# Modulation products in steps of four, and one weight split for two k-tiles

## The chip, the cores and the metric

The kernel runs on one core of one Trainium2 chip. The metric is device time in microseconds (us) per execution. The engines named below are TensorE (PE, with its weight loads PEld), VectorE (DVE), ScalarE (ACT), GpSimd (POOL) and the queue of SyncE (SP), which issues nearly all loads.

## The reference, cut to what matters

Two transformer blocks are applied to 256 rows of 2048 numbers, in float32. The first block has two layers; each multiplies normalised rows by a wide input matrix, runs three kinds of attention and multiplies by an output matrix. Its rows are modulated first, by a scale and a shift that come from two conditioning vectors:

```python
shift, scale, gate = jnp.split(sc @ w_ada[l] + b_ada[l], 3, axis=-1)
shift_c, scale_c, gate_c = jnp.split(scc @ w_ada[l] + b_ada[l], 3, axis=-1)
h = rms(x, norm_w[l]) * (1.0 + scale[:, None]) + shift[:, None]
hc = rms(xc, norm_w[l]) * (1.0 + scale_c) + shift_c
u = h @ w_in
```

So the first layer's scale and shift need two rows (`sc` and `scc`, each of 2048 numbers) times 2048 x 4096 weights, before the first dense product. The second block is a mixer, a cross attention and a feed-forward layer, all of them dense products of 256 rows with wide matrices.

## The kernel before, in words

**Dense products.** A weight matrix comes in chunks of at most 512 columns, and a chunk in blocks of two k-tiles (a k-tile is 128 rows). `weights` (line 388) loads one block of 128x1024 numbers on the SP queue into a `raw` tile, of which there are three. Each k-tile is then split in two: `split` (line 374) writes `hi` on ScalarE (line 376) and `lo` = raw - hi on VectorE (line 377). There are four `hi` tiles and four `lo` tiles of 128x512, so four k-tiles can be held. `dense` (line 403) streams the split weights and holds the activations still, `denseT` (line 429) holds the weights still and streams the activations; both make three products for each k-tile and token tile or column tile (lines 420 to 422, and 440, 442, 443). With 512 tokens (four token tiles: the first layer and the keys of the second) a block is 24 products of 512 columns. With 256 tokens it is 12 products of up to 512 columns in `dense`, or 24 of 256 columns in `denseT`; that is the second layer's queries, and all of the second block. Results leave PSUM through an `evac` function at the end of a chunk.

**The first products.** `first_products` (line 1310) works through the 16 k-tiles of the first three chunks of `w_in` in five parts of 2, 2, 4, 4 and 4 k-tiles (`PARTS`), since a part of the rows can be normalised as soon as its scale and shift are known. While the dense products of one part run, the modulation of the next part is made by `ada_pe` (line 601): 16 steps, one for each k-tile of `w_ada`, and an `end`. A step loads the weights of one k-tile and makes two products (shift and scale) at line 629. The stationary operand is 32 columns wide (the two conditioning vectors and zeros), so a product uses one of four groups of 32 columns of the array, and its result goes to the 32 PSUM partitions that belong to the group: `q = 64 * (kt % 2) + 32 * b`. The products are 256 columns long in the first two parts (the two lie side by side in one loaded tile) and 512 in the last three (one loaded tile each). The loaded tiles are those of the attention's `PT`, five of them. The steps of the first part are called directly in `block1`, between the loads of `x` and `ctx` (line 1371).

**What sets the order.** `push` queues jobs and `tick` starts them at a pace in modelled TensorE time; in `first_products` one job starts every `n * len(chunks) * 2.56 / FIRST` us of it. A scheduler then puts the instructions of each engine in a fixed order, also the SP queue's loads; at run time each engine works through its list and waits where an operand or a buffer is not free.

Of the kernel before, what the change touches and what calls it, by code (L numbers as in the profile page):

```python
# [11 lines left out]
F32R = mybir.dt.float32r  # L12
# [2 lines left out]
AX = mybir.AxisListType  # L15

UNITS = 50
FIRST = 20
D = 2048
NKT = D // 128  # L20
EPS = 1e-6
# [121 lines left out]
class Weights:  # L143


    def __init__(self, ap, name):
        self.ap, self.at, o = ap, {}, 0
        rows, chunks = CHUNKS[name]
        for ch in chunks:
            self.at[tuple(ch)] = o  # L150
            o += rows * sum(n for _, n in ch)
# [41 lines left out]
class K:  # L193
# [8 lines left out]
    def __init__(self, ctx, tc, a):  # L202
        self.tc, self.nc, self.a = tc, tc.nc, a
        nc = self.nc
        self.jobs, self.running, self.next = [], [], 0.0
        self.urgent, self.asked, self.unext = [], 0, 0.0
        self.side, self.side_rate, self.side_credit = [], 0.0, 0.0
        self.now, self.late = 0.0, []
        self.const = ctx.enter_context(tc.tile_pool(name="const", bufs=1))
        self.str = ctx.enter_context(tc.tile_pool(name="stream", bufs=3))  # L210
        self.up = ctx.enter_context(tc.tile_pool(name="units", bufs=1))
        self.sm = ctx.enter_context(tc.tile_pool(name="small", bufs=8))
        self.ps = ctx.enter_context(tc.tile_pool(name="psum", bufs=1, space=bass.MemoryType.PSUM))
        self.nu = self.alt = 0
        self.vt = self.const.tile([128, NVT], F32, name="vt")
        nc.scalar.dma_start(self.vt, a["vt"])
        n = CS["tri"][0]
        self.cs = self.const.tile([128, n], F32, name="cs")
        nc.scalar.dma_start(self.cs, a["cst"][:, :n])
        self.flip = self.const.tile([128, 128], F32, name="flip")  # L220
        nc.scalar.dma_start(self.flip, a["flip"])
        self.ident = self.const.tile([128, 128], F32, name="ident")
        make_identity(nc, self.ident)
        self.ones = self.const.tile([128, 128], F32, name="ones")
        nc.vector.memset(self.ones, 1.0)
        self.mhalf = self.const.tile([128, 16], F32, name="mhalf")
        nc.vector.memset(self.mhalf, -0.5)
# [161 lines left out]
    def weights(self, w, k0, pieces):  # L389

        nc = self.nc
        raw = self.str.tile([128, 2, 512], F32, name=self.name("raw"), tag="raw", bufs=3)
        n, src = w.block(k0, pieces)
        nc.sync.dma_start(raw[:, :, :n], src)
        out = []
        for j in range(2):
            hi = self.str.tile([128, 512], F32R, name=self.name("hi"), tag="hi", bufs=4)
            lo = self.str.tile([128, 512], F32R, name=self.name("lo"), tag="lo", bufs=4)
            self.split(hi[:, :n], lo[:, :n], raw[:, j, :n])
            out.append((hi, lo))  # L400
        return out

    def dense(self, act, kts, w, pieces, cols, evac, what="d", skip={}):

# [173 lines left out]
class Block1(K):  # L578
# [27 lines left out]
    def ada_pe(self, k0, n, cst, done):  # L606


        nc = self.nc
        w = self.a["w_ada"]  # L610
        W = 128 * n
        st = {}

        def step(kt):
            if kt == 0:
                st[0] = self.psum("o", "ada")
            acc = st[0]
            at = w.offset + k0 * 128 * D * 2 + kt * 128 * 2 * W
            if 2 * W <= 512:
                raw = self.temp("raw", tag="PT", bufs=5)  # L620
                nc.sync.dma_start(raw[:, :2 * W], bass.AP(tensor=w.tensor, offset=at, ap=[[2 * W, 128], [1, 2 * W]]))
                raws = raw[:, :W], raw[:, W:2 * W]
            else:
                raws = [self.temp("raw", tag="PT", bufs=5) for _ in range(2)]
                for b in range(2):
                    nc.sync.dma_start(raws[b], bass.AP(tensor=w.tensor, offset=at + b * W, ap=[[2 * W, 128], [1, W]]))
            for b in range(2):
                q = 64 * (kt % 2) + 32 * b
                nc.tensor.matmul(acc[q:q + 32, :W], lhsT=cst[:, kt, :], rhs=raws[b], start=kt < 2,
                                 stop=kt >= NKT - 2, skip_group_check=True)  # L630

        def end():
            sb = self.temp("ada")
            nc.scalar.activation(sb[:, :W], st[0][:, :W], AF.Copy)
            pt = self.psum("t", "ada")
            for j in range(n):
                nc.tensor.transpose(pt[:, 128 * j:128 * j + 128], sb[:, 128 * j:128 * j + 128], self.ident)
            pv = pt[:, :W].rearrange("p (j h b r) -> p b r j h", j=n, h=2, b=2)
            out = self.ada_tile(0)[:, :, :, k0:k0 + n]
            for b in (1, 0):  # L640
                nc.vector.tensor_reduce(out[:, b], pv[:, b, 0:2], op=OP.add, axis=AX.X)
            self.finish_ada(0, k0, n)
            done()

        return [lambda kt=kt: step(kt) for kt in range(NKT)] + [end]

    def ada_steps(self, l, b0, nb, streams):

# [662 lines left out]
    def first_products(self, h, w, chunks):  # L1311
# [14 lines left out]
        for i, (k0, n) in enumerate(PARTS):  # L1326
            if i + 1 < len(PARTS):
                for f in steps(i + 1):
                    self.push(f)
            self.every = n * len(chunks) * 2.56 / FIRST  # L1330
            for pieces, put, dst in chunks:
# [5 lines left out]
    def block1(self):  # L1337
        nc, a, tc = self.nc, self.a, self.tc
        with ExitStack() as es:
# [27 lines left out]
            first = self.ada_pe(*PARTS[0], self.cst, lambda: None)  # L1367
            pt = self.psum("s", "rb")
            for i, (x, src) in enumerate(loads):
                nc.sync.dma_start(x, src)  # L1370
                first[i]()
                if i % 4 == 3:
                    r = self.rstd(self.sumsq(X[i // 4]), 1, D)
                    if i == len(loads) - 1:
                        first[-1]()
                    self.row(pt, i // 4, r)
# [554 lines left out]
```

## Time and profile before

| | us |
|---|---|
| median of 3 runs | 3529.87 (3525.9 to 3531.43) |
| the profiled execution | 3528.03 |
| its span in the trace | 3526.3 |
| PE busy | 3420.2 (97%) |
| DVE busy | 2299.7 (65%) |
| ACT busy | 1785.4 (51%) |
| mean granted TensorE clock | 0.983 |

A busy share is a mean over the whole span. Matmuls overlap in the pipeline, so a TensorE that reads as fully busy can still lose time between them: what a product costs is read from the starts of two neighbours, not from its duration. A group's idle time and what ended it stand behind its busy time. In the trace one product of the modulation is two matmul records.

### The profile page before, as it was taken

How to read it: one execution, taken by the hardware profiler on the slowest of the kernel's cores; microseconds unless marked ns; L12 is line 12 of the kernel's file. 1: busy time of each engine (PE TensorE's matmuls, PEld its weight loads, DVE VectorE, ACT ScalarE, POOL GpSimd, SP SyncE). 2: the span in 40 equal slices, each digit the busy share in tenths (PEclk: the TensorE clock that was granted, in tenths of full speed). 3: DMA queues.
4: the chain of work that ended last, by engine and by line, in shares of the span. 5: the costliest groups of instructions: out<-in, count | busy, mean ns of one | idle time of the engine just before them, and what ended most of it. 6: DMA issues, size and time to landing. Idle time of an engine off the chain costs nothing.

```text
span 3526.3 us, 57200 instructions
## 1 busy us (share of the span) xinstructions
PE 3420.2 (97%) x20842; PEld 2952.3 (84%) x20842; DVE 2299.7 (65%) x4939; ACT 1785.4 (51%) x3554; POOL 321.7 (9%) x472
## 2 busy tenths in 40 slices
PE   8999999999999998999999999999999899999998
PEld 3467778888787888887777999999978899999886
DVE  2359889868876475887673555555566766666554
ACT  3235556336525355766463445444555555555544
POOL 0012221103110031111110000000000000000000
PEclk9999999999999999999998999999999999999999
DMA  7745544642465434445544535555655455555555
GB/s 257 228 147 172 140 129 132 210 161 73 145 212 182 156 115 134 144 154 156 161 151 137 186 116 184 184 181 186 197 177 169 147 184 183 183 185 190 194 192 166
DMA packets 226778, 590.45 MB, mean 167 GB/s; under 512 B 39904, under 2 KB 63184, under 8 KB 226496
## 3 DMA queue, kind: packets, MB, share of 16 engines
q1 hardware_dynamic: 221104, 570.41, 50.6%
q0 software_dynamic: 4864, 15.69, 1.4%
q8 instruction: 163, 2.67, 0.3%
q14 instruction: 119, 0.97, 0.1%
q10 hardware_dynamic: 528, 0.71, 0.1%
HBM read 582.48 MB, written 4.24 MB: 166 GB/s over the span
## 4 chain that ended last, share of the span: by engine, by line
PE 54%; issue 12%; DVE 4%; ACT 1%; POOL 1%; DMA 1%; POOLq 0%; SPq 0%; DVEq 0%; ACTq 0%
PE upd L442 5%; PE upd L440 5%; PE upd L443 5%; PE downd L420 2%; PE downd L422 2%; PE downd L421 2%; PE L0outd L420 1%; PE L0outd L422 1%; PE L0outd L421 1%; PE Ss L529 1%; DVE lo L377 1%; PE oo L572 1%; PE vd L420 1%; PE vd L422 1%; PE vd L421 1%
## 5 line engine op out<-in xcount | busy, mean ns | idle before, releaser
L377 DVE TENSOR_TENSOR lo<-raw,hi 128x512 fp32r<-128x512 f32 (+3 forms) x1788 | 1204.5, 679 | 892.0 <-ACT hi L376 886.1
L376 ACT ACTIVATE hi<-raw 128x512 fp32r<-128x512 f32 (+3 forms) x1788 | 1089.7, 614 | 1299.7 <-PE upd L442 190.8
L440 PE MATMUL upd<-hi,hi 128*128 128x256 f32 x1408 | 399.2, 284 | 0.0
L442 PE MATMUL upd<-lo,hi 128*128 128x256 f32 x1408 | 399.1, 283 | 0.0
L443 PE MATMUL upd<-hi,lo 128*128 128x256 f32 x1408 | 398.8, 283 | 0.0
L668 DVE SCALAR_TENSOR_TENSOR scr<-raw,cb 128x512 f32<-128x512 f32 x448 | 297.4, 692 | 26.0 <-DMA raw<-in_w_ada_dram 13.4
L442 PEld LDWEIGHTS upd<-lo,hi 128*128 128x128 f32 x1408 | 270.8, 192 | 0.3 <-DVE lo L484 0.3
L443 PEld LDWEIGHTS upd<-hi,lo 128*128 128x128 f32 x1408 | 270.8, 192 | 0.0
L440 PEld LDWEIGHTS upd<-hi,hi 128*128 128x128 f32 x1408 | 270.7, 192 | 0.0
L355 POOL TENSOR_TENSOR sm<-sm,mhalf 128x2 f32<-128x2 f32 (+4 forms) x116 | 116.7, 1008 | 1401.9 <-DVE sm L354 1396.3
L420 PE MATMUL downd<-hi,hi 128*128 128x512 f32 x352 | 137.7, 391 | 0.0
L422 PE MATMUL downd<-hi,lo 128*128 128x512 f32 x352 | 137.7, 391 | 0.0
L421 PE MATMUL downd<-lo,hi 128*128 128x512 f32 x352 | 137.6, 391 | 0.0
L540 ACT ACTIVATE P<-Ss,sm 128x512 f32<-128x512 f32 (+1 forms) x164 | 99.5, 607 | 67.7 <-DVE sm L536 45.9
L364 ACT ACTIVATE PT<-pTt 128x256 f32<-128x256 f32 x226 | 79.1, 380 | 63.6 <-PE pTt L557 56.2
L420 PE MATMUL L0outd<-hi,hi 128*128 128x512 f32 x256 | 101.2, 395 | 4.3 <-DVE ot L1290 3.0
L443 PE MATMUL L0zd<-hi,lo 128*128 128x512 f32 x256 | 99.7, 392 | 0.9 <-DVE lo L377 0.9
L440 PE MATMUL L0zd<-hi,hi 128*128 128x512 f32 x256 | 100.3, 392 | 0.0
L536 DVE TENSOR_REDUCE sm<-Ss 128x1 f32<-128x512 f32 (+1 forms) x164 | 95.6, 586 | 7.2 <-PE Ss L529 6.3
L442 PE MATMUL L0zd<-lo,hi 128*128 128x512 f32 x256 | 100.1, 391 | 0.0
L421 PE MATMUL L0outd<-lo,hi 128*128 128x512 f32 x256 | 100.1, 391 | 0.0
L422 PE MATMUL L0outd<-hi,lo 128*128 128x512 f32 x256 | 99.3, 391 | 0.2 <-DVE lo L377 0.2
(568 smaller groups left out, 9006.2 us busy)
## 6 DMA issues: line engine op xcount, KB each, us to landing
raw<-in_w_in_dram SPq DMA_DIRECT2D x344, 512.0 KB, 3.5
raw<-in_w_ada_dram SPq DMA_DIRECT2D x384, 256.0 KB, 3.1
raw<-in_ffn_w_up_dram SPq DMA_DIRECT2D x176, 512.0 KB, 3.5
raw<-in_w_out_dram SPq DMA_DIRECT2D x104, 512.0 KB, 4.2
raw<-in_ffn_w_down_dram SPq DMA_DIRECT2D x88, 512.0 KB, 3.9
raw<-in_w_proj_b_dram SPq DMA_DIRECT2D x32, 512.0 KB, 3.7
raw<-in_w_in_dram SPq DMA_DIRECT2D x32, 288.0 KB, 3.3
raw<-in_w_proj_a_dram SPq DMA_DIRECT2D x16, 512.0 KB, 4.3
```

Source lines behind the costliest of these rows:

```text
L355: nc.gpsimd.tensor_tensor(r, ms, self.mhalf[:, :n], op=OP.pow)
L376: self.nc.scalar.activation(hi, src, AF.Copy)
L377: self.nc.vector.tensor_sub(lo, src, hi.bitcast(F32))
L420: nc.tensor.matmul(ps[t][:, a], lhsT=xh, rhs=hi[:, a], start=first, stop=False)
L421: nc.tensor.matmul(ps[t][:, a], lhsT=xh, rhs=lo[:, a], start=False, stop=False)
L422: nc.tensor.matmul(ps[t][:, a], lhsT=xl, rhs=hi[:, a], start=False, stop=last)
L440: nc.tensor.matmul(p, lhsT=hi[:, s], rhs=xh, start=kt == 0 and c % per == 0, stop=False, skip_group_check=True)
L442: nc.tensor.matmul(p, lhsT=hi[:, s], rhs=xl, start=False, stop=False, skip_group_check=True)
L443: nc.tensor.matmul(p, lhsT=lo[:, s], rhs=xh, start=False, stop=kt == nk - 1, skip_group_check=True)
L536: nc.vector.tensor_reduce(nm[:, 0:1], S[:, :nk], op=OP.max, axis=AX.X, negate=True)
L540: nc.scalar.activation(P[:, :nk], S[:, :nk], AF.Exp, bias=nm[:, 0:1], accum_out=nm[:, 1:2])
L668: nc.vector.scalar_tensor_tensor(self.temp("scr"), raw, 1.0, st[s], op0=OP.mult, op1=OP.mult, accum_out=st["p"][:, s, k, q:q + 1])
```

## The change: what it does

`weights` takes two `hi` and two `lo` tiles of 128x2x512 in place of four of 128x512 each, and splits both k-tiles of a block with one instruction on ScalarE and one on VectorE. A step of `ada_pe` now takes two k-tiles: it makes all its loads (two or four) and then four products, one in each group of 32 columns. The loaded tiles rotate over eight places, five of tag `PT` and three of tag `P`. A part has 8 steps and an `end` in place of 16 and an `end`, and `FIRST` goes from 20 to 11, so that a job starts about half as often. In `block1` a step follows every second load.

```diff
-FIRST = 20
+FIRST = 11
...
-        out = []
-        for j in range(2):
-            hi = self.str.tile([128, 512], F32R, name=self.name("hi"), tag="hi", bufs=4)
-            lo = self.str.tile([128, 512], F32R, name=self.name("lo"), tag="lo", bufs=4)
-            self.split(hi[:, :n], lo[:, :n], raw[:, j, :n])
-            out.append((hi, lo))
-        return out
+        hi, lo = (self.str.tile([128, 2, 512], F32R, name=self.name(x), tag=x, bufs=2) for x in ("hi", "lo"))
+        self.split(hi[:, :, :n], lo[:, :, :n], raw[:, :, :n])
+        return [(hi[:, j], lo[:, j]) for j in range(2)]
...
+        def tile():
+            self.ada_at = (self.ada_at + 1) % 8
+            return self.temp("raw", tag="P", bufs=3) if 4 <= self.ada_at < 7 else self.temp("raw", tag="PT", bufs=5)
+
-        def step(kt):
-            if kt == 0:
+        def step(kt0):
+            if kt0 == 0:
                 st[0] = self.psum("o", "ada")
             acc = st[0]
...
+            raws = {}
+            for kt in (kt0, kt0 + 1):
...
-            for b in range(2):
+            for kt, b in raws:
                 q = 64 * (kt % 2) + 32 * b
-                nc.tensor.matmul(acc[q:q + 32, :W], lhsT=cst[:, kt, :], rhs=raws[b], start=kt < 2,
+                nc.tensor.matmul(acc[q:q + 32, :W], lhsT=cst[:, kt, :], rhs=raws[kt, b], start=kt < 2,
                                  stop=kt >= NKT - 2, skip_group_check=True)
...
-        return [lambda kt=kt: step(kt) for kt in range(NKT)] + [end]
+        return [lambda kt=kt: step(kt) for kt in range(0, NKT, 2)] + [end]
...
-                first[i]()
+                if i % 2:
+                    first[i // 2]()
```

What stands in the engines' lists, at three places. First TensorE, in the fourth part of the first products, while the modulation of the last part is made. Before (`adao` is the modulation's PSUM tile, `L0firstd` that of a dense product):

```order
L422 MATMUL L0firstd_1371<-hi_1381,lo_1167 128x512
L629 MATMUL adao_1235<-raw_1406,cstat_130 32x512
L629 MATMUL adao_1235<-raw_1407,cstat_130 32x512
L420 MATMUL L0firstd_1372<-hi_1381,hi_1166 128x512
L421 MATMUL L0firstd_1372<-lo_1382,hi_1166 128x512
L422 MATMUL L0firstd_1372<-hi_1381,lo_1167 128x512
L420 MATMUL L0firstd_1373<-hi_1381,hi_1166 128x512
L421 MATMUL L0firstd_1373<-lo_1382,hi_1166 128x512
L422 MATMUL L0firstd_1373<-hi_1381,lo_1167 128x512
L629 MATMUL adao_1235<-raw_1418,cstat_130 32x512
L629 MATMUL adao_1235<-raw_1419,cstat_130 32x512
```

The same place now:

```order
L418 MATMUL L0firstd_1173<-hi_1257,lo_1228 128x512
L632 MATMUL adao_1183<-raw_1308,cstat_130 32x512
L632 MATMUL adao_1183<-raw_1310,cstat_130 32x512
L632 MATMUL adao_1183<-raw_1312,cstat_130 32x512
L632 MATMUL adao_1183<-raw_1314,cstat_130 32x512
L416 MATMUL L0firstd_1173<-hi_1257,hi_1271 128x512
L417 MATMUL L0firstd_1173<-lo_1258,hi_1271 128x512
L418 MATMUL L0firstd_1173<-hi_1257,lo_1272 128x512
```

The two products that stood between dense products have become four. In the parts before it the scheduler keeps fewer of them together. Uninterrupted groups of modulation products, counted through both lists, for the parts whose modulation is made (the first part's stand among the loads of `x`):

| modulation of part | columns | products | groups before | groups now |
|---|---|---|---|---|
| second | 256 | 32 | 16 | 10 |
| third | 512 | 32 | 24 | 20, one of five |
| fourth | 512 | 32 | 18 | 16 |
| fifth | 512 | 32 | 15 | 7, one of eight |

Second, ScalarE at the end of a chunk of the mixer's output product (`wo2d`, 256 tokens). Before (`sq` is the evacuation's sum of squares, one for each token tile):

```order
L376 ACTIVATE hi_28052<-raw_28050 128x512
L376 ACTIVATE hi_28056<-raw_28050 128x512
L1431 ACTIVATE sq_28040,sm_27543<-wo2d_27862 128x512
L376 ACTIVATE hi_28074<-raw_28072 128x512
L1431 ACTIVATE sq_28044,sm_27544<-wo2d_27863 128x512
L376 ACTIVATE hi_28078<-raw_28072 128x512
```

And now:

```order
L376 ACTIVATE hi_25724<-raw_25722 128x1024
L1435 ACTIVATE sq_25712,sm_25279<-wo2d_25566 128x512
L1435 ACTIVATE sq_25716,sm_25280<-wo2d_25567 128x512
L376 ACTIVATE hi_25742<-raw_25740 128x1024
L376 ACTIVATE hi_25760<-raw_25758 128x1024
```

The next chunk's second block was split in two instructions, one on either side of the second `sq`; now its one instruction stands behind both.

Third, the SP queue, where the third block of `w_in` (`raw_474` in both lists) stands among the loads of the modulation. Before:

```order
L394 DMA raw_400<-in_w_in_dram 128x1024
L621 DMA raw_413<-in_w_ada_dram 128x512
L621 DMA raw_420<-in_w_ada_dram 128x512
L621 DMA raw_427<-in_w_ada_dram 128x512
L621 DMA raw_434<-in_w_ada_dram 128x512
L394 DMA raw_474<-in_w_in_dram 128x1024
```

And now:

```order
L394 DMA raw_400<-in_w_in_dram 128x1024
L623 DMA raw_409<-in_w_ada_dram 128x512
L623 DMA raw_411<-in_w_ada_dram 128x512
L623 DMA raw_423<-in_w_ada_dram 128x512
L623 DMA raw_425<-in_w_ada_dram 128x512
L623 DMA raw_440<-in_w_ada_dram 128x512
L623 DMA raw_442<-in_w_ada_dram 128x512
L623 DMA raw_454<-in_w_ada_dram 128x512
L623 DMA raw_456<-in_w_ada_dram 128x512
L394 DMA raw_474<-in_w_in_dram 128x1024
```

Eight loads of the modulation stand ahead of it where four stood.

## Rows read from the trace of the kernel before

**Rows 1.** Windows: modulation of the second to fifth part; the start; the mixer.

```profile
core 0: us, PE busy (x) PEld busy (x) DVE busy (x) ACT busy (x) POOL busy (x), PEclk, DMA share, GB/s
36.10:62.60 26.50, 26.50 (x128) 14.51 (x129) 6.88 (x16) 10.01 (x19) 0.00 (x0) 1.00 0.72 231
62.60:115.00 52.40, 51.12 (x169) 18.09 (x168) 17.72 (x33) 9.48 (x20) 0.00 (x0) 1.00 0.62 192
115.00:167.60 52.60, 52.60 (x214) 29.52 (x213) 21.81 (x40) 13.93 (x27) 0.00 (x0) 1.00 0.75 249
167.60:213.50 45.90, 45.85 (x193) 23.43 (x192) 16.27 (x30) 9.66 (x17) 1.45 (x2) 1.00 0.70 231
20.00:30.00 10.00, 8.70 (x38) 2.52 (x35) 0.62 (x4) 5.08 (x16) 1.09 (x2) 0.50 1.05 391
1850.00:1900.00 50.00, 49.80 (x165) 37.31 (x166) 14.98 (x21) 13.61 (x22) 1.82 (x2) 0.69 0.28 90
```

**Rows 2.** Timeline of TensorE: a group of two 256-column modulation products (start, us).

```profile
45.18 0.40 PE L422 MATMUL L0firstd<-hi,lo 128*128 128x512 f32 x1
45.51 0.63 PE L629 MATMUL adao<-raw,cstat 128*32 128x256 f32 x4
...
46.40 0.39 PE L421 MATMUL L0firstd<-lo,hi 128*128 128x512 f32 x1
```

**Rows 3.** The same timeline: a group of one 512-column product.

```profile
72.83 0.40 PE L422 MATMUL L0firstd<-hi,lo 128*128 128x512 f32 x1
73.16 1.04 PE L629 MATMUL adao<-raw,cstat 128*32 128x512 f32 x2
...
74.47 0.39 PE L421 MATMUL L0firstd<-lo,hi 128*128 128x512 f32 x1
```

**Rows 4.** The same timeline: a group of four 512-column products.

```profile
167.52 0.39 PE L422 MATMUL L0firstd<-hi,lo 128*128 128x512 f32 x1
167.84 1.06 PE L629 MATMUL adao<-raw,cstat 128*32 128x512 f32 x8
...
169.17 0.39 PE L421 MATMUL L0firstd<-lo,hi 128*128 128x512 f32 x1
```

**Rows 5.** DMA issues: size, median us to landing.

```profile
raw<-in_w_in_dram SPq DMA_DIRECT2D x344, 512.0 KB, 3.5
raw<-in_w_ada_dram SPq DMA_DIRECT2D x384, 256.0 KB, 3.1
```

**Rows 6.** Groups by shape: the splits (busy us, mean ns).

```profile
L376 ACT ACTIVATE hi<-raw 128x512 fp32r<-128x512 f32 x1608 | 1008.3, 630 | 1197.8 <-PE upd L442 190.8 <-DVE lo L377 173.6 <-PE L0firstd L422 85.6
L376 ACT ACTIVATE hi<-raw 128x384 fp32r<-128x384 f32 x68 | 34.3, 522 | 43.4 <-PE L1qbd L422 11.2 <-PE L1zd L442 7.1 <-PE L0zd L442 6.5
L377 DVE TENSOR_TENSOR lo<-raw,hi 128x512 fp32r<-128x512 f32 x1608 | 1117.0, 700 | 836.8 <-ACT hi L376 832.2 <-PE L0zd L442 2.0 <-DMA raw<-in_w_ada_dram 0.7
L377 DVE TENSOR_TENSOR lo<-raw,hi 128x384 fp32r<-128x384 f32 x68 | 37.2, 567 | 26.5 <-ACT hi L376 25.5 <-PE toTs L826 0.9
```

**Rows 7.** Timelines of PE, ACT and DVE: one k-tile of the mixer's output product.

```profile
2605.90 0.40 PE L420 MATMUL wo2d<-hi,hi 128*128 128x512 f32 x1
2606.14 0.40 PE L421 MATMUL wo2d<-lo,hi 128*128 128x512 f32 x1
2606.10 0.63 ACT L376 ACTIVATE hi<-raw 128x512 fp32r<-128x512 f32 x1 [0.76 <-PE wo2d L422]
2606.77 0.69 DVE L377 TENSOR_TENSOR lo<-raw,hi 128x512 fp32r<-128x512 f32 x1 [0.70 <-ACT hi L376]
```

**Rows 8.** Timeline of ACT: the end of a chunk there.

```profile
2610.29 0.60 ACT L1431 ACTIVATE sq<-wo2d 128x512 f32<-128x512 f32 x1 [0.76 <-PE wo2d L422]
...
2610.98 0.64 ACT L376 ACTIVATE hi<-raw 128x512 fp32r<-128x512 f32 x1
```

**Rows 9.** Waits of TensorE: us in total, times, longest.

```profile
PE L1qbd L420 <- ACT hi L376: 5.1, 1, 5.1
PE L0cqd L421 <- DVE lo L377: 3.9, 2, 3.2
```

More of the change, by code (lines that the diff above doesn't have):

```diff
@@ L213, in __init__ @@
         self.ps = ctx.enter_context(tc.tile_pool(name="psum", bufs=1, space=bass.MemoryType.PSUM))
-        self.nu = self.alt = 0
+        self.nu = self.alt = self.ada_at = 0
         self.vt = self.const.tile([128, NVT], F32, name="vt")
@@ L612, in ada_pe @@
         st = {}
-        def step(kt):
-            if kt == 0:
+        def tile():
[3 more added lines that the diff above has]
+            if kt0 == 0:
                 st[0] = self.psum("o", "ada")
             acc = st[0]
[L618 to L624, printed above, removed]
+            raws = {}
+            for kt in (kt0, kt0 + 1):
+                at = w.offset + k0 * 128 * D * 2 + kt * 128 * 2 * W
+                if 2 * W <= 512:
+                    raw = tile()
+                    nc.sync.dma_start(raw[:, :2 * W], bass.AP(tensor=w.tensor, offset=at, ap=[[2 * W, 128], [1, 2 * W]]))
+                    raws[kt, 0], raws[kt, 1] = raw[:, :W], raw[:, W:2 * W]
+                    continue
                 for b in range(2):
-                    nc.sync.dma_start(raws[b], bass.AP(tensor=w.tensor, offset=at + b * W, ap=[[2 * W, 128], [1, W]]))
-            for b in range(2):
+                    raws[kt, b] = tile()
+                    nc.sync.dma_start(raws[kt, b], bass.AP(tensor=w.tensor, offset=at + b * W,
+                                                           ap=[[2 * W, 128], [1, W]]))
+            for kt, b in raws:
                 q = 64 * (kt % 2) + 32 * b
-                nc.tensor.matmul(acc[q:q + 32, :W], lhsT=cst[:, kt, :], rhs=raws[b], start=kt < 2,
+                nc.tensor.matmul(acc[q:q + 32, :W], lhsT=cst[:, kt, :], rhs=raws[kt, b], start=kt < 2,
                                  stop=kt >= NKT - 2, skip_group_check=True)
```

## Prediction

> **What bounds the kernel now.** I read the windows by stretch first: TensorE is busy without a break in the stretches in which the modulation is made (26.50 of 26.50 us, 52.60 of 52.60 and so on), while VectorE and ScalarE are below half and the transfers take 62 to 75% of the DMA engines' time [rows 1]. Over the whole span it is the same: 97% busy in the table. So time saved on TensorE's list counts in full, and time saved on ScalarE or VectorE counts only where TensorE waits for them. Then I read TensorE's timeline around the products of line 629, since a busy share says nothing of what they cost, then the splits by shape, the timelines of a stage with 256 tokens, and last who TensorE waits for.
>
> **The modulation's products: what a group costs.** Two dense products of 512 columns start 0.23 us apart [rows 7]. Around a group of two 256-column products, L422 starts at 45.18 and the second dense product behind the group at 46.40: 1.22 us in place of 2 x 0.23, so the group costs 0.76 us [rows 2]. With one 512-column product it is 74.47 - 72.83 = 1.64, less 0.46: 1.18 us [rows 3]. With four, one in each group of 32 columns, it is 169.17 - 167.52 = 1.65 us, so 1.19 [rows 4]. One product and four cost the same: the four groups of columns work side by side, and what is paid for is the group. A fifth product in a row finds its columns in use; from the durations I estimate 1.0 us more for it, and as much for the second four of an eight.
>
> The Trainium skill weighs against this ("TensorE: Matmul & The Clock Gate", Part 3): three column tiles of 32 columns measured 2.38 times the speed of one after the other, not three times. By that efficiency four products would stream for some 1.25 us in place of 1.0, an estimate from the page; about 13 groups of four would give back 3 us of the gain below. The trace does not agree: eight records took 0.01 us more than two [rows 3, 4], so the sum goes by the rows.
>
> **The sum for the modulation.** The groups are counted in the table under the change. Second part: 16 groups become 10, 6 x 0.76 = 4.6 us less. Third: 24 x 1.18 = 28.3 becomes 20 x 1.18 + 1.0 = 24.6, 3.7 less. Fourth: two groups fewer, 2.4 less. Fifth: 15 x 1.18 = 17.7 becomes 7 x 1.18 + 1.0 = 9.3, 8.4 less. Together 19 us. It is not the halving that the change speaks of, since the scheduler leaves many fours in pieces (in the third and fourth part they stand as two, one and one). The first part's steps stand under the loads of `x` and `ctx`, where the DMA engines are full (share 1.05, 391 GB/s from 20 to 30 us [rows 1]); the same bytes are loaded, so I count 0 there, between -1 and +1.
>
> What could fail to follow: the four stretches move about 40 MB (each rate by its length) in 177 us. In 158 us that is 252 GB/s, and in the last stretch (45.9 - 8.4 us) 283, against the 391 that the start reaches [rows 1], so the loads need not become the bound. On the SP queue the third block of `w_in` stands behind eight modulation loads now, the last of which waits for a tile that the fourth step sets free. Counted through TensorE's list with the costs above, that is some 9 us before the block's first use; a load lands in 3.5 us [rows 5], its split takes 2.3 (below), 3 us remain. Later blocks have more. A step's loads start when the step two before it is done, also some 9 us ahead of use, against 3.1 to land [rows 5]. So 0 for waits here, up to +10 if the queue runs late.
>
> **The split for two k-tiles.** `hi` of 128x512 takes 0.630 us and of 128x384 0.522; `lo` 0.700 and 0.567 [rows 6]. A straight line through them gives 1.06 and 1.23 for 1024 (upper bound: twice the half, 1.26 and 1.40; lower bound: the slope alone, 0.86 and 1.06). Some 890 pairs save up to 0.2 us each on either engine, all of it beside TensorE: worth nothing by itself.
>
> What counts is when the split is ready. Before, a k-tile's split starts as soon as one of four tiles is free, so two k-tiles are ready ahead. Now it starts when a whole pair is done, and the other pair is all that is ahead. In the mixer's output product a k-tile begins at 2605.90, and the `hi` that its predecessor set free starts at 2606.10, 0.20 later; `lo` follows 0.04 after `hi` ends [rows 7]. For a pair: 0.20 + 1.06 + 0.04 + 1.23 = 2.53 us. The pair in work lasts 12 x 0.23 = 2.76, and the first `lo` is needed one product later, at 2.99. That is 0.46 to spare; by the upper bounds (2.90) still 0.09. So in the steady state TensorE does not wait, neither here nor where the pair is 24 products (`denseT`, or 512 tokens, where it lasts twice as long). The `raw` tile is free at 2.5 us instead of about 1.6, so its next load has 6 us instead of 7, against 3.5 [rows 5].
>
> Where something stands in front, it no longer hides. (a) Chunk ends of the three output products of the second block: the second `sq` can start at 0.20 and holds ScalarE for 2610.98 - 2610.29 = 0.69 [rows 8]; `hi` then ends at 1.95 and `lo` at 3.22, 0.23 late. Eleven such ends: +2.5 us. (b) Narrow pairs: for 384 columns (the second layer's queries, 16 pairs) the line gives 0.20 + 0.84 + 0.04 + 0.97 = 2.05 against 12 x 0.17 + 0.17 = 2.2; for 264 columns (the mixer's first two chunks, 16 pairs) 1.6 against 1.6. Nothing is to spare, and other work stands on both engines. Between 0 and 0.45 us each (the upper bound, twice the half) I take 0.2: +6 us. (c) In the first layer a pair lasts twice as long, so it has 3 us to spare, and VectorE has less to do. Its waits for splits are few (the longest group is 3.9 us [rows 9]); I take -3, between -5 and +5.
>
> Sum: -19 + 2.5 + 6 - 3 = -13.5 us. The profiled execution took 3528.0 us, of which 3526.3 is span; its median run is 1.8 us longer. 3529.9 - 13.5 = 3516.
>
> **Rivals.** *The spare time is gone (slower).* In the second layer, at the mixer's start, in its output product and the cross attention about 190 pairs have 256 tokens and attention or normalisation work between their splits. One VectorE instruction of 0.70 us that falls in front of a `lo` leaves it 0.24 late, in all of them 46 us. It decides against the change from an average of 0.11 us on (20 us together). For it: the 0.46 above, and the queries already wait 5.1 us in one place [rows 9]. Against it: between two `lo` VectorE has 1.6 us of its own in each pair, so most of that work fits without being in front. With all 46 it would be 3516 + 46 = 3562.
>
> *The groups of four wait for their loads.* A group holds TensorE until the last of four tiles is there, and the queue holds weight blocks behind them. For it: 283 GB/s asked of the last stretch. Against it: two steps of lead. Then 5 us remain of 19: 3529.9 - 5 + 5.5 = 3530.
>
> *The lists get better as a whole.* VectorE has up to 150 us less to do (890 x 0.17); where it is the later engine of an attention stage, TensorE's waits fall. For it: VectorE is at 65% over the span. Against it: the waits for splits are short [rows 9]. Perhaps 15 us more: 3500.
>
> The granted clock is a spread under all of them: TensorE had 0.69 of full speed from 1850 to 1900 us while it was busy [rows 1], and a moved wait can shift such a spell by some 10 us either way.
>
> **How the numbers follow.** The forecast has 0.62 and its own range is 3505 to 3528; slower by lost spare time 0.14, waits for loads 0.13, better lists 0.11. A change of 0.2%, 7 us, is what a measurement of this kernel can tell. Faster (below 3522.8): 0.9 of 0.62, all of 0.11 and a little of the loads' case: 0.70. Within: 0.18. Slower: nearly all of 0.14, less what ends within: 0.12. The range reaches from the better lists to the near half of the slower case: 3497 to 3545.
>
> **What would show it.** In the profile after, the modulation's products should stand in groups of eight records that cost 1.2 us, and the first layer's first dense products should end some 19 us earlier, with TensorE still without breaks and DMA near 0.8. `hi` of 128x1024 near 1.06 us and `lo` near 1.23. Waits for `lo` and `hi` should show at the chunk ends of the output products and in the 384- and 264-column chunks, and be absent from the feed-forward products. The prediction is wrong if the first products end less than 10 us earlier, or if waits for splits add up to more than 25 us.

## The result

The changed kernel takes 3553.8 us (median of 4 runs, 3552.5 to 3560.1), the kernel before 3529.8 in the same comparison: a ratio of 1.0073, with a 95% interval of 1.0056 to 1.0091. It is 24 us slower where 13.5 us less was forecast. The profiled execution, the longest of the four, took 3560.05 us, with a span of 3557.9 against 3526.3 before: by these two spans the loss is 31.6 us, by the medians 24.

| | before | after |
|---|---|---|
| PE busy, us | 3420.2 | 3419.8 |
| DVE busy, us | 2299.7 | 2187.0 |
| ACT busy, us | 1785.4 | 1636.3 |
| mean granted TensorE clock | 0.983 | 0.982 |
| TensorE's listed waits for `hi` and `lo` of lines 376 and 377, summed, us | 24.5 | 47.2 |

TensorE does the same work, VectorE and ScalarE are busy for 113 and 149 us less, and the time rises. So the busy time that was saved is not what the kernel waited for; TensorE waits longer for the results of these two engines than before.

### The profile page after: what moved, and what is told of

Read it like the earlier page. It is cut to its first block, busy times and chain, and to the rows that moved or that the text cites. A ratio compares the mean times of both kernels' runs of the same rounds, so it can differ in the third digit from the quotient of the medians.

```text
span 3557.9 us, 54261 instructions
## 1 busy us (share of the span) xinstructions
PE 3419.8 (96%) x20842; PEld 2958.2 (83%) x20842; DVE 2187.0 (61%) x4045; ACT 1636.3 (46%) x2664; POOL 320.2 (9%) x472
## 5 line engine op out<-in xcount | busy, mean ns | idle before, releaser
L377 DVE TENSOR_TENSOR lo<-raw,hi 128x1024 fp32r<-128x1024 f32 (+3 forms) x894 | 1063.9, 1191 | 981.7 <-ACT hi L376 974.1
L376 ACT ACTIVATE hi<-raw 128x1024 fp32r<-128x1024 f32 (+3 forms) x894 | 917.1, 1026 | 1356.6 <-PE upd L438 198.5
L364 ACT ACTIVATE PT<-pTt 128x256 f32<-128x256 f32 x226 | 78.9, 380 | 84.5 <-PE pTt L553 75.7
```

The lines of the kernel that those rows point to most:

```text
L376: self.nc.scalar.activation(hi, src, AF.Copy)
L377: self.nc.vector.tensor_sub(lo, src, hi.bitcast(F32))
```

## The profile after

The modulation does what was worked out. TensorE's timeline around a group of eight records (the columns are those of [rows 4]):

```profile
171.20 0.40 PE L418 MATMUL L0firstd<-hi,lo 128*128 128x512 f32 x1
171.52 1.07 PE L632 MATMUL adao<-raw,cstat 128*32 128x512 f32 x8
172.52 0.50 PE L416 MATMUL L0firstd<-hi,hi 128*128 128x512 f32 x1
172.85 0.39 PE L417 MATMUL L0firstd<-lo,hi 128*128 128x512 f32 x1
```

From the dense product before the group to the second behind it 1.65 us, less 2 x 0.23: 1.19 us for the group, as in [rows 4]. The windows of the second to fifth part, of the stretch of low clock in [rows 1], and of the feed-forward's first product (columns as in [rows 1]):

```profile
36.80:62.00 25.20, 25.20 (x143) 15.02 (x142) 8.70 (x17) 12.42 (x21) 0.00 (x0) 1.00 0.73 240
62.00:102.00 40.00, 40.00 (x138) 15.54 (x136) 9.84 (x13) 2.75 (x4) 0.00 (x0) 1.00 0.67 218
102.00:159.00 57.00, 55.09 (x234) 31.22 (x232) 26.45 (x48) 16.37 (x27) 0.00 (x0) 1.00 0.70 236
159.00:206.00 47.00, 46.68 (x229) 30.40 (x229) 22.39 (x36) 12.70 (x20) 3.52 (x4) 1.00 0.75 238
1850.00:1900.00 50.00, 49.17 (x184) 36.78 (x182) 22.00 (x35) 22.56 (x42) 8.45 (x6) 0.80 0.31 101
2790.00:3301.00 511.00, 511.00 (x4243) 510.70 (x4242) 322.21 (x406) 255.82 (x310) 2.18 (x4) 1.00 0.56 182
```

TensorE stays busy while the modulation is made, and the DMA engines are not full (0.67 to 0.75). In the feed-forward, 511 us long, it does not stop at all. The splits by shape, to be read beside [rows 6]:

```profile
L377 DVE TENSOR_TENSOR lo<-raw,hi 128x1024 fp32r<-128x1024 f32 x804 | 989.8, 1232 | 923.3 <-ACT hi L376 915.9 <-PE exs L1546 1.3
L376 ACT ACTIVATE hi<-raw 128x1024 fp32r<-128x1024 f32 x804 | 851.6, 1059 | 1258.2 <-PE upd L438 198.5 <-PE downd L418 134.6 <-PE L0zd L438 97.0
```

1.06 and 1.23 us: the straight line holds to the rounding. The chain of a pair in the mixer's output product, the place of [rows 7], on ScalarE and VectorE:

```profile
2605.51 1.06 ACT L376 ACTIVATE hi<-raw 128x1024 fp32r<-128x1024 f32 x1 [1.73 <-PE wo2d L418]
2608.28 1.06 ACT L376 ACTIVATE hi<-raw 128x1024 fp32r<-128x1024 f32 x1 [1.72 <-PE wo2d L418]
...
2606.60 1.23 DVE L377 TENSOR_TENSOR lo<-raw,hi 128x1024 fp32r<-128x1024 f32 x1 [1.57 <-ACT hi L376]
```

`hi` starts every 2.77 us and `lo` ends 2.32 us behind `hi`'s start: the chain that the forecast added up. The prices that were read from rows came out: the group, the two splits, the chain. Part of the loss stands in the waits, which answer to [rows 9]:

```profile
PE rbt L491 <- POOL sm L355: 11.4, 4, 4.3
PE adao L632 <- DVE cstat L1364: 8.7, 1, 8.7
PE trs L464 <- DVE h L474: 8.2, 6, 2.7
PE trs L464 <- DVE x L1454: 6.3, 3, 2.7
PE L1qbd L416 <- ACT hi L376: 5.4, 1, 5.4
PE L0zd L439 <- DVE lo L377: 4.8, 2, 2.4
PE L0cqd L417 <- DVE lo L377: 4.5, 1, 4.5
```

`L0zd` is a stage of the first layer, with 512 tokens. Before, its two waits were short:

```profile
PE L0zd L443 <- DVE lo L377: 0.9, 2, 0.7
```

One of its two waits now, first on TensorE, then on VectorE and ScalarE:

```profile
643.10 0.39 PE L438 MATMUL L0zd<-lo,hi 128*128 128x512 f32 x1
645.93 0.50 PE L439 MATMUL L0zd<-hi,lo 128*128 128x512 f32 x1 [2.44 <-DVE lo L377]
```

```profile
639.04 0.69 DVE L671 SCALAR_TENSOR_TENSOR scr<-raw,cb 128x512 f32<-128x512 f32 x1
639.65 0.09 DVE L671 DVE_READ_ACCUMULATOR scr<-raw,cb 128x1 f32 x1
643.42 0.69 DVE L671 SCALAR_TENSOR_TENSOR scr<-raw,cb 128x512 f32<-128x512 f32 x1 [3.68 <-POOL kpr L736]
644.04 0.08 DVE L671 DVE_READ_ACCUMULATOR scr<-raw,cb 128x1 f32 x1
644.04 0.69 DVE L671 SCALAR_TENSOR_TENSOR scr<-raw,cb 128x512 f32<-128x512 f32 x1
644.65 0.08 DVE L671 DVE_READ_ACCUMULATOR scr<-raw,cb 128x1 f32 x1
644.65 1.22 DVE L377 TENSOR_TENSOR lo<-raw,hi 128x1024 fp32r<-128x1024 f32 x1
```

```profile
637.41 1.06 ACT L376 ACTIVATE hi<-raw 128x1024 fp32r<-128x1024 f32 x1 [0.27 <-PE L0zd L438]
```

This place shows how a wait comes about. `hi` is done at 638.47, so `lo` could start then. In VectorE's list it stands behind instructions of another job (line 671, the next layer's modulation), and these behind one that GpSimd releases late: 3.68 us in which VectorE does nothing. `lo` starts 6.2 us after it could. A pair lasts 24 x 0.227 = 5.4 us here, and TensorE stands for 2.6 (645.93 - 643.10 - 0.23). The same stretch of work in the kernel with the old split and the new modulation steps (`ada_only` below), on VectorE:

```profile
627.81 0.21 DVE L996 TENSOR_TENSOR kpr<-kpe,rows 128x64 f32<-128x64 f32 x1
627.94 0.68 DVE L377 TENSOR_TENSOR lo<-raw,hi 128x512 fp32r<-128x512 f32 x1
...
629.44 0.69 DVE L675 SCALAR_TENSOR_TENSOR scr<-raw,cb 128x512 f32<-128x512 f32 x1 [0.21 <-POOL kpr L740]
```

A `lo` of one k-tile stands ahead of the job's instructions here, and GpSimd is waited for 0.21 us. TensorE does not stop.

Why GpSimd is late is in its own list. In the changed kernel it makes tables for the next layer (lines 707 to 718) ahead of `kpr`, and waits for the load of their `rows` first:

```profile
639.41 0.63 POOL L711 TENSOR_TENSOR rCqb<-cs,rows 128x128 f32<-128x128 f32 x1 [2.91 <-DMA rows<-in_rows_dram]
...
643.07 0.31 POOL L736 TENSOR_TENSOR kpr<-kpr,rt 128x64 f32<-128x64 f32 x1
```

In `ada_only` the same `kpr` stands ahead of the tables:

```profile
627.96 1.44 POOL L740 TENSOR_TENSOR kpr<-kpr,rt 128x64 f32<-128x64 f32 x1 [3.60 <-DVE rt L736]
...
633.59 0.45 POOL L715 TENSOR_TENSOR rCqb<-cs,rows 128x128 f32<-128x128 f32 x1 [3.60 <-DMA rows<-in_rows_dram]
```

So the new split gave the scheduler other sizes and counts of tiles, and it put even GpSimd's list in another order. Of the kernels in the table below, the tables stand in front in all seven that have pairs or three single tiles, and VectorE waits 1.9 to 3.7 us there; in the four with four or five single tiles they stand behind, and it waits 0.2 us at most.

## The experiments

Each kernel was timed in five rounds against the kernel before on the same chip; that one's median was 3525.0, 3526.6 and 3529.3 in the three comparisons, so kernels of different ones are set against each other by their ratios. The stages' lengths are those of its profiled execution: the first column is the end of the last dense product of `first_products`, the next three run to the end of the last product of the first layer's output, of the second layer's output, and of the mixer's `vs`; then from the end of `pb` to the end of `xo` (the mixer's output product and the cross attention); the last column is the rest up to the last product, which ends 14.5 us before the span in every kernel. The lengths are of one execution each, and executions of one kernel differ by up to 16 us.

| kernel | median, us | ratio to before (95%) | first | layer 1 | layer 2 | mixer's start | `wo2` to `xo` | rest |
|---|---|---|---|---|---|---|---|---|
| before | 3529.8 | 1 | 255.2 | 841.6 | 662.5 | 70.2 | 206.4 | 1475.9 |
| after | 3553.8 | 1.0073 (1.0056 to 1.0091) | 239.4 | 854.8 | 684.3 | 77.7 | 213.3 | 1473.9 |
| `split_only` | 3573.8 | 1.0134 (1.0121 to 1.0147) | 255.3 | 854.0 | 681.4 | 77.6 | 214.6 | 1473.6 |
| `ada_only` | 3500.3 | 0.9931 (0.9916 to 0.9946) | 227.5 | 841.1 | 662.3 | 69.5 | 206.2 | 1472.0 |
| `halves_in_pair` | 3522.5 | 0.9994 (0.9985 to 1.0004) | 227.3 | 851.8 | 669.5 | 75.1 | 209.0 | 1471.6 |
| `hi_whole` | 3539.0 | 1.0038 (1.0024 to 1.0051) | 230.3 | 848.1 | 678.5 | 76.7 | 211.3 | 1480.8 |
| `lo_whole` | 3550.3 | 1.0069 (1.0054 to 1.0083) | 237.8 | 856.6 | 676.8 | 78.4 | 210.3 | 1469.4 |
| `three_singles` | 3539.9 | 1.0037 (1.0023 to 1.0052) | 243.0 | 848.0 | 675.3 | 75.0 | 209.3 | 1474.6 |
| `after_four` | 3545.1 | 1.0057 (1.0044 to 1.0070) | 226.2 | 855.4 | 681.3 | 78.1 | 214.5 | 1469.2 |
| `ada_four` | 3493.7 | 0.9912 (0.9896 to 0.9927) | 225.5 | 841.0 | 661.8 | 70.2 | 207.6 | 1470.4 |
| `five_singles` | 3579.1 | 1.0148 (1.0135 to 1.0161) | 227.9 | 842.5 | 678.4 | 78.9 | 215.4 | 1519.8 |

**The two parts apart.** `ada_only` is the changed kernel with this:

```diff
-        hi, lo = (self.str.tile([128, 2, 512], F32R, name=self.name(x), tag=x, bufs=2) for x in ("hi", "lo"))
-        self.split(hi[:, :, :n], lo[:, :, :n], raw[:, :, :n])
-        return [(hi[:, j], lo[:, j]) for j in range(2)]
+        out = []
+        for j in range(2):
+            hi = self.str.tile([128, 512], F32R, name=self.name("hi"), tag="hi", bufs=4)
+            lo = self.str.tile([128, 512], F32R, name=self.name("lo"), tag="lo", bufs=4)
+            self.split(hi[:, :n], lo[:, :n], raw[:, j, :n])
+            out.append((hi, lo))
+        return out
```

> The kernel before with the change to the modulation steps and FIRST alone; the split as before (one instruction for each k-tile, four hi and four lo tiles). Theory (the merged split costs everything that was lost): the first products end earlier and nothing behind them gives it back. With this split TensorE's list holds 9, 17 (one of five), 8 (one of five) and 7 (one of eight) groups for the second to fifth part, where the changed kernel has 10, 20, 16 and 7: against before 7 x 0.76 + 7 x 1.18 - 0.9 + 10 x 1.18 - 0.9 + 8 x 1.18 - 0.9 = 32 us less, so 3530 - 32 = 3498 (3492 to 3508). Rival (what was lost came from the earlier and denser start, by spells of the lower clock or by the order of the attention stages behind it): 3535 to 3555, with the stages behind the first products longer by 30 us or more.

3500.3 us, with the first products' end at 227.5 and every later stage as long as before, within 1 us up to the mixer. Behind the first products the lists of TensorE, VectorE, ScalarE and GpSimd are in the same order as before. `split_only` is the kernel before with the same lines the other way round.

> The kernel before with the merged split alone (two hi and two lo tiles of 128x2x512, one instruction on each engine for two k-tiles); modulation steps and FIRST as before. Theory (the merged split costs what was lost): in the changed kernel the first products end 16 us earlier and the end is 31.6 us later, so 47 us were lost behind them; here 3530 + 47 = 3577 (3560 to 3590). Rival (the loss came from the modulation steps): 3525 to 3537. If the two parts only cost together, it lies between.

3573.8 us, by the ratio 47 above the kernel before. Its stages behind the first products are those of the changed kernel: 854.0 and 854.8, 681.4 and 684.3, 77.6 and 77.7, and the lists are in the same order there. The whole loss is the merged split's, wherever the first products end.

**Tiles or instructions.** The merged split changes two things: a pair of tiles comes free as a whole, and an instruction holds its engine for twice as much. `halves_in_pair` keeps the first and undoes the second:

```diff
-        self.split(hi[:, :, :n], lo[:, :, :n], raw[:, :, :n])
+        for j in range(2):
+            self.split(hi[:, j, :n], lo[:, j, :n], raw[:, j, :n])
```

> The changed kernel with the pair tiles kept (two hi, two lo of 128x2x512), but split by two instructions on either engine, one for each k-tile, as before. Theory of the buffers (a pair's tile comes free only when both k-tiles are done, and that is where the spare time goes): no better than the changed kernel, 3545 to 3560. Theory of the long instruction (attention and normalisation work on ScalarE and VectorE stands behind splits of 1.0 and 1.2 us in place of 0.6 and 0.7): the loss goes, and with the modulation's groups of this list (those of the kernel with the old split) 3498 to 3510. In between, each has a share.

3522.5: in between. Against `ada_only` the pairs cost 22 us (0.0063 in the ratio), with the first products as early; against the changed kernel the short instructions give back 28 (0.0079), and in the traces 12 us of that lie in the first products. At the place shown above VectorE waits for GpSimd here too, but less, and `lo` comes in two pieces:

```profile
633.81 0.69 DVE L672 SCALAR_TENSOR_TENSOR scr<-raw,cb 128x512 f32<-128x512 f32 x1 [2.74 <-POOL kpr L737]
...
635.04 1.29 DVE L377 TENSOR_TENSOR lo<-raw,hi 128x512 fp32r<-128x512 f32 x2
```

```profile
635.78 0.50 PE L440 MATMUL L0zd<-hi,lo 128*128 128x512 f32 x1 [1.12 <-DVE lo L377]
```

TensorE goes on at 635.78, when the first k-tile's `lo` is done, while the second is still in work; it waited 1.12 us in place of 2.44. GpSimd is 0.94 us less late here, and the `lo` that TensorE needs is 0.5 us shorter; both are in the difference. The Trainium skill states this as a rule ("Perfetto Trace Analysis", Optimizing Scalar/DVE Operations): where ScalarE and VectorE are not saturated but cause gaps on other engines, breaking instructions up may let work be done sooner; grouping into larger ones is for an engine that is saturated. VectorE was busy for 65% of the span before and ScalarE for 51%, and the runs agree with it.

**Which engine.** `hi_whole` and `lo_whole` are the changed kernel with the long instruction on one engine and two halves on the other:

```diff
-        self.split(hi[:, :, :n], lo[:, :, :n], raw[:, :, :n])
+        self.nc.scalar.activation(hi[:, :, :n], raw[:, :, :n], AF.Copy)
+        for j in range(2):
+            self.nc.vector.tensor_sub(lo[:, j, :n], raw[:, j, :n], hi[:, j, :n].bitcast(F32))
```

> The changed kernel with one instruction for two k-tiles on ScalarE alone; VectorE splits in two instructions, into halves of the same pair tiles. With two instructions on both engines (halves_in_pair) it took 3522, with one on both 3554, of which 12 us are the modulation's groups: 39 of them where the old split's list has 41 less... counted in the lists behind the first part: 41 groups with two instructions on both, 51 in the changed kernel, 42 here. Theory (VectorE's long instruction costs, since VectorE is the fuller of the two engines, 66% against 51%): about 3525 (3520 to 3532). Rival (ScalarE's long one costs, since both halves of lo now wait for the whole hi): 3540 to 3550.

> The changed kernel with one instruction for two k-tiles on VectorE alone; ScalarE splits in two instructions, into halves of the same pair tiles. Behind the first part the list has 53 groups of modulation products (41 with two instructions on both engines, 51 in the changed kernel), some 12 us more in the first products. Theory (VectorE's long instruction costs): 3545 to 3555. Rival (ScalarE's costs): 3522 + 12 = 3534 (3530 to 3540).

(Behind the first part the lists hold 53 groups in the changed kernel, 44 and 55 in these two and 55 in `three_singles`; where an expectation has 51, 42 and 53, it counts two too few.) 3539.0 and 3550.3. `lo_whole` came out as expected of VectorE's cost, `hi_whole` met neither figure: 14 us above one and just below the other. So the theory that VectorE's instruction alone costs falls. By the sums of the stages behind the first products, the long `hi` adds 18 us to `halves_in_pair` (half of it in the rest), the long `lo` 15, and both together 22 to 27 (`after_four`, after); by the ratios, less the first products, it is 13, 16 and 16 to 23. So each of the two costs. That they do not add up is likely, but single executions and intervals of 5 us do not settle it.

**How many k-tiles ahead.** `three_singles` is `ada_only` with three `hi` and three `lo` tiles:

```diff
-            hi = self.str.tile([128, 512], F32R, name=self.name("hi"), tag="hi", bufs=4)
-            lo = self.str.tile([128, 512], F32R, name=self.name("lo"), tag="lo", bufs=4)
+            hi = self.str.tile([128, 512], F32R, name=self.name("hi"), tag="hi", bufs=3)
+            lo = self.str.tile([128, 512], F32R, name=self.name("lo"), tag="lo", bufs=3)
```

> The modulation change with the old split (ada_only), and three hi and three lo tiles of one k-tile each in place of four: while one k-tile is worked on, two are ahead, as many as the pairs leave in the worst case (three with four tiles). The list has 53 groups of modulation products behind the first part against 41: 2 x 0.76 to 12 x 1.18, some 13 us. Theory of the buffers (the k-tiles ahead are what the pairs lost): 3500 + 13 + 20 to 25 behind the first products = 3533 to 3540. Rival (pairs cost for another reason, the tiles ahead do not matter): 3500 + 13 = 3513.

3539.9, the upper end. The first products end 15.5 us later, and behind them 31 us are lost in the profile's spans (3539.7 - 3493.1 - 15.5) and 22 by the ratios (37 - 15.5), with no long instruction and no pair. So fewer split k-tiles ahead cost by themselves, or by the order of the lists that comes with them: here too the tables stand ahead of `kpr`, and VectorE waits 2.74 us there. From the end of `vs` to the end of `xo` the order is nearly that of `ada_only` (826 of VectorE's 831 instructions), TensorE spends the same 30.7 us at its lower clock, and the stretch is 5.6 us longer (917.3 against 911.7); there it is the tiles. In the layers, where most of the loss is, no run has new tiles with the old order, so the shares of the two stay open.

The other direction, with one `raw` tile given for it, is `five_singles`, built on `ada_four` (below):

```diff
-        raw = self.str.tile([128, 2, 512], F32, name=self.name("raw"), tag="raw", bufs=3)
+        raw = self.str.tile([128, 2, 512], F32, name=self.name("raw"), tag="raw", bufs=2)
...
-            hi = self.str.tile([128, 512], F32R, name=self.name("hi"), tag="hi", bufs=4)
-            lo = self.str.tile([128, 512], F32R, name=self.name("lo"), tag="lo", bufs=4)
+            hi = self.str.tile([128, 512], F32R, name=self.name("hi"), tag="hi", bufs=5)
+            lo = self.str.tile([128, 512], F32R, name=self.name("lo"), tag="lo", bufs=5)
```

> ada_four with five hi and five lo tiles of one k-tile in place of four, paid for with one raw tile (two in place of three). Theory (what counts is how many split k-tiles stand ahead): going from four to three tiles cost 31 us behind the first products; a fourth k-tile ahead gives back a part of the 25 us that TensorE still waits for splits there: 3482 to 3490 against 3494. Rival (with two raw tiles the next load starts too late, and the loads become what is waited for): 3497 to 3520.

3579.1: the rival, and worse than it said. ScalarE's waits:

```profile
ACT hi L376 <- DMA raw<-in_w_in_dram: 439.6, 219, 9.4
ACT hi L376 <- DMA raw<-in_ffn_w_up_dram: 195.8, 133, 2.4
ACT hi L376 <- DMA raw<-in_ffn_w_down_dram: 120.0, 75, 2.9
```

With two `raw` tiles the split waits for its load all along, and the feed-forward, which takes 766.5 to 769.9 us in every other kernel, takes 798.9. A fourth split k-tile ahead is therefore not tested by itself, nor are three pairs tried.

**The groups of the modulation.** In `ada_four`, which is `ada_only` with one edit more, the product on the tile that is loaded last stands first in each step, and the others are kept behind it:

```diff
-            for kt, b in raws:
+            def product(kt, b):
                 q = 64 * (kt % 2) + 32 * b
-                nc.tensor.matmul(acc[q:q + 32, :W], lhsT=cst[:, kt, :], rhs=raws[kt, b], start=kt < 2,
+                return nc.tensor.matmul(acc[q:q + 32, :W], lhsT=cst[:, kt, :], rhs=raws[kt, b], start=kt < 2,
...
+            *others, last = raws
+            landed = product(*last)
+            with self.tc.issue_after(landed.ins):
+                for kb in others:
+                    product(*kb)
```

> The modulation change with the old split (ada_only), and in each step the product on the tile that is loaded last stands first in TensorE's list and the other three behind it, so that the fours stay together more often: 33 groups of modulation products behind the first part where ada_only has 41; the third part has 8 (one of six, one of eight) in place of 17. By the price of a group: 9 x 1.18 - 0.9 - 0.3 = 9.4 us less in the third part, one group more in the fourth: 3500 - 8 = 3492 (3487 to 3499). Rival (waiting for the last load of a step holds TensorE as long as the pieces cost): 3498 to 3506.

3493.7, the fastest kernel of all, though its interval overlaps that of `ada_only`, so that its lead over that one is not shown. The first products end 2.0 us earlier where 8 were expected. The third part ends with a group that waits:

```profile
83.87 1.07 PE L637 MATMUL adao<-raw,cstat 128*32 128x512 f32 x8 [0.97 <-DMA raw<-in_w_ada_dram]
88.47 1.94 PE L637 MATMUL adao<-raw,cstat 128*32 128x512 f32 x8 [3.53 <-DMA raw<-in_w_ada_dram]
```

```profile
84.00:96.00 12.00, 7.68 (x30) 4.17 (x27) 2.34 (x8) 2.67 (x5) 0.00 (x0) 0.58 0.92 328
```

TensorE has used up its dense products by 84 us and stands for the loads, which run at 328 GB/s with the DMA engines at 0.92; then it works at the lower of its two clocks (a granted share of 0.5) for most of the stretch (0.58 on average). The groups' gain is there until the loads are the bound. The same edit in the changed kernel is `after_four`:

> The changed kernel, split as it is (one instruction on either engine for two k-tiles), and in each modulation step the product on the tile that is loaded last stands first in TensorE's list with the other three behind it. Behind the first part the list has 32 groups in place of 53: the third part 8 (one of six, one of eight) for 20, the fourth 7 (one of eight) for 16. Theory (12 us of what the merged split cost lie in the first products, because the order that it gives breaks the fours): the first products end near 226, as in ada_four (225.5), in place of 239.4, and the rest stays: 3554 - 13 = 3541 (3535 to 3547). Rival (the merged split slows the first products by itself, by waits for hi and lo): first products end at 235 or later, 3548 to 3556.

The first products end at 226.2, as the theory has it, and the time is 3545.1, at its upper end. By the ratio (0.0016) 6 of the 13 us arrive at the end, but the two intervals overlap, so that even these 6 are not shown. The merged split delays the first products by the order that the scheduler makes of it (53 groups of products in the changed kernel, 32 here), not by waits for `hi` and `lo`.

## Why the prediction was wrong

**The modulation (-19 us): right in the mechanism, short by 3.** The first products end 15.8 us earlier (255.2 to 239.4); they also begin 1.4 later, at 37.5 in place of 36.1, which is just outside the 0 +- 1 that was set for the loads at the start. That four products cost what one does, and that groups are what is paid, holds in `ada_only` too: with 41 groups its first products end 27.7 us earlier, where the price of a group gave 32. Loads held nothing up in the changed kernel, as forecast; they do in `ada_four`, where TensorE asks for them sooner.

**The steady state of the split (0): right.** The chain is 2.5 us against 2.77 for a pair, and in the feed-forward TensorE does not stop for 511 us.

**Term (c), the first layer (-3 us): the step that failed, and (b) failed by it too.** It said that a pair of 512 tokens lasts twice as long and so has 3 us to spare, and that VectorE has less to do. The first layer became 13.2 us longer (854.8 against 841.6). The 3 us were counted from the split's own chain, as if `hi` and `lo` began when a tile is free. In these stages they begin when VectorE and ScalarE come to them, and what stands ahead can wait for another engine: 3.68 us for GpSimd in the one place shown, by an order of the lists that the new split itself brought. That the order of the lists would change behind the first products was given no term. The reserve against such a wait is the k-tiles that stand split. Before, a freed tile was split again at once, so up to three stood ahead of the one in work; with pairs it is two as long as the second of a pair is in work, and they are made as a pair. The forecast read the waits as few from the longest one, 3.9 us; summed they were 24.5 already before, where its sign of being wrong was more than 25. Now they are 47.2.

**Term (b), with (a): the second layer and the mixer, +8.5 in all.** The second layer lost 21.8 us, the mixer's start 7.5, its output product and the cross attention 6.9: 36.2 together, the larger part of the miss. The chunk ends themselves were priced high: the waits of `wo2d` for `lo` come to 1.3 us, and the other two output products have none. The 0.2 us for each narrow pair was a price for narrow chunks; what the stages share is attention and normalisation between their splits, whatever the width. In the second layer TensorE's listed waits grow from 28 to 43 us, those for `hi` and `lo` from 11 to 21; that each comes about as in the place shown is inferred, not looked up.

**The rival "the spare time is gone" was the case**, with its sign and its cause (work in front of a `lo`). It was given 0.14 and 46 us, and the loss behind the first products is 47 in the spans (31.6 later at the end, 15.8 earlier at 239) and 40 by the medians. That the figures are so close is luck: it was placed in the 256-token pairs alone, and 13.2 us lie in the first layer. The argument against it, that VectorE's other work fits between two `lo` (1.6 us, which is 1.5 by 2.76 - 1.23), counted busy time. In the place shown the engine was not busy; it stood waiting in its list.

By the ratios the changed kernel stands 50 us behind `ada_only` (0.0142): 22 for the pairs of tiles, 22 for the long instructions with the modulation's groups in order (`after_four` against `halves_in_pair`), 6 for the groups that they break; each of the three is uncertain by some 7 us. How the first two reach TensorE is shown in part: the listed waits grow by 27 us from `ada_only` (94.6) to the changed kernel (121.9), 21 of them for `hi` and `lo`. The mean granted clock goes from 0.986 to 0.982; the lower clock is half the full one, so the time at it is 2 x 0.018 x 3557.9 = 128 us in place of 2 x 0.014 x 3493.1 = 98. Of the 98 us, 17 lie ahead of the end of the first products, and of the 128 none, so behind them it is 128 in place of 81, which costs up to 23 us more. Whether these stretches follow from the waits is open: they lie in the stages that wait, but `lo_whole` has the same listed waits (121.5) and a mean clock of 0.988, and no run holds one fixed and moves the other.

## What to carry to other kernels

Where a product is fed by engines that also do other work, the time that a feeding step can be late is set by the number of finished tiles ahead of the consumer. Hold it against the longest idle stretch in those engines' lists, not against their busy share. Merging instructions on engines that are not full saved nothing here and cost readiness: what is freed and delivered in larger pieces is freed and delivered later. And when an edit changes sizes or counts of tiles, compare the order of every engine's list, and count what it does to parts of the kernel that the edit does not touch: GpSimd's tables came to stand ahead of `kpr`, and 12 of the 28 us that the modulation gained in the first products were lost to the order that the split brought.

## What was not expected of the hardware

Products in different groups of 32 columns cost the same for one, two or four: 1.18 to 1.19 us for a group of 512 columns, before and after. The one group of eight in the changed kernel costs 2.05 us, so the second four cost 0.86, where the forecast took 1.0.

The merged instruction saves less than two durations less one. `halves_in_pair` shows two halves in a row in the mixer's output product, where the changed kernel has 1.06 and 1.23:

```profile
2561.57 1.15 ACT L376 ACTIVATE hi<-raw 128x512 fp32r<-128x512 f32 x2 [1.57 <-PE wo2d L419]
2562.23 1.29 DVE L377 TENSOR_TENSOR lo<-raw,hi 128x512 fp32r<-128x512 f32 x2 [1.44 <-ACT hi L376]
```

1.15 and 1.29 us, not 1.26 and 1.40: neighbours overlap, and the merged form saves 0.09 us on ScalarE and 0.06 on VectorE. The Trainium skill ("Perfetto Trace Analysis", Optimizing Scalar/DVE Operations) gives some 93 and 60 ns for each instruction, with about twice that in a single instruction's profiled time. The trace agrees on what is saved, 0.09 and 0.06 us. Two durations of single instructions less the merged one are 0.20 and 0.17 us, about twice the page's figure on ScalarE and nearly three times on VectorE.
